# A decoder trunk in one kernel: three layer norms take the form of the last one, with mean and scale left in PSUM

## The chip, the core and the metric

The kernel runs on one core of a Trainium2 chip, as one program in one launch. The core has a matrix engine (PE in the profile, with its weight loads as PEld), VectorE (DVE), ScalarE (ACT), GpSimd (POOL) and a queue for DMAs on SyncE (SP). The metric is the time of one execution on the device in microseconds, and the median over several runs is compared.

## The reference, cut to what matters

Two token groups (256 prompt tokens, and 8 sequences with one token each) go through the same two layers; the kernel keeps all 264 tokens side by side. Each layer has a feed-forward half-step, a mixer and another feed-forward half-step, each followed by a layer norm over 1024 features:

```python
def layer_norm(x, g, b):
    mu = jnp.mean(xf, axis=-1, keepdims=True)
    var = jnp.mean(jnp.square(xf - mu), axis=-1, keepdims=True)
    return ((xf - mu) * lax.rsqrt(var + LN_EPS) * g + b)
...
x = layer_norm(DN_ALPHA * x + 0.5 * swiglu(x, wg1, wu1, wd1), g[0], b[0])
x = layer_norm(DN_ALPHA * x + Mixer(x), g[1], b[1])
x = layer_norm(DN_ALPHA * x + 0.5 * swiglu(x, wg2, wu2, wd2), g[2], b[2])
```

That makes six norms, numbered 0 to 5 here as in the code (`ln`): layer 0 has norms 0, 1 and 2, layer 1 has 3, 4 and 5. The mixer of layer 0 is attention beside an RWKV recurrence, that of layer 1 is a state space (S5) with a gated output projection. Everything is float32.

## The kernel before

Activations lie with features on partitions: 1024 features are 8 blocks (k = 0 to 7) of 128 partitions x 264 tokens. Each float32 product is made of three matmuls on operands that are split into a high and a low part (`block`, lines 297 to 299: high x high, high weight x low activation, low weight x high activation). Weights come from HBM in chunks of up to 8 blocks of 128x128; `Stream.take` loads each ahead and splits it: ScalarE makes the high part (`wh`, line 199), VectorE the low part (`wl`, line 200). So both engines have one large instruction for each chunk all through the kernel, 317 chunks in all. The split chunks lie in 4 buffers, and a new split can start only when PE is done with the oldest.

The order of instructions on each engine is set when the kernel is built: a planner goes through the program with costs of its own, gives instructions that come earlier in the program precedence when several are ready, and writes one fixed order for each engine. On the chip each engine then works through its order and waits wherever an operand isn't there yet. The same source lines therefore can stand in another order at another norm.

How a norm is made. While the projection before it runs, `put_r` (called once for each of the 8 output blocks m) adds the residual to the projection (line 348), takes off a first estimate of the mean, and sums the blocks and their squares in `acc` and `sq`. At the last block four matmuls with a matrix of 1/1024 leave in two PSUM tiles what is still missing of the mean (`dl`) and the mean square (`var`), spread over all partitions (lines 372 and 373). For norms 0, 1, 2 and 4 `put_r` also writes `rh` and `rl`, the two parts of g * r, with r not yet normalised.

Then `stats` makes of these the two factors of the norm. ScalarE squares `dl` (line 394), VectorE takes the square off `var` into the SBUF tile `rstd` (line 396), ScalarE takes the root (line 397) and copies -`dl` into the SBUF tile `nmu` (line 399), VectorE takes the reciprocal in place (line 401). The blocks are centered by `center` (line 437), r + `nmu`: block 0 on VectorE, blocks 1, 2-3, 4-5 and 6-7 on GpSimd in four instructions. Both operands lie in SBUF. Later `unit` (line 448) multiplies a block by `rstd` on VectorE, `norm_block` (line 441) has ScalarE apply g and b, and `split_block` splits the result into `xh` (ScalarE, line 453) and `xl` (VectorE, line 454) for the matmuls.

What hides a norm. `ffn` starts its first three pairs of column blocks (six PSUM banks, `raw`) on `rh` and `rl`, which needs nothing of the norm but r; the factors are put in afterwards on the six finished banks by `fix` (lines 469, 471 and 472: a copy of two columns, `nmu` times one of them plus the bank, and the product with `rstd`). While PE is at these 144 matmuls, the other engines normalise and split the 8 blocks. The fourth pair (`pg`, `pu`) needs `xh` and `xl`, and its bank is that of the first `raw` tile, which line 471 has to have read.

The last norm (5) has nothing to hide behind and goes through `finish`: `dl` and `var` stay in PSUM; ScalarE copies the mean to SBUF for GpSimd, which centers blocks 7, 6 and 5 (line 417); VectorE centers blocks 0 and 1 against `dl` (line 421), writes the reciprocal back into `var` (line 422), and centers blocks 2 to 4 as it comes to them (line 426) before the product with `var` (line 427).

Of the kernel before, what the change touches and what calls it, by code (L numbers as in the profile page):

```python
# [9 lines left out]
F32 = mybir.dt.float32  # L10
# [3 lines left out]
AF = mybir.ActivationFunctionType  # L14
ALU = mybir.AluOpType
# [6 lines left out]
NT = NP + NB  # L22
# [198 lines left out]
class Trunk:  # L221
# [164 lines left out]
        with self.tc.issue_after(after.ins):  # L386
            self.nc.scalar.activation(self.eps[:, 2:3], self.eps[:, 0:1], func)

    def stats(self):

        nc = self.nc
        tt = nc.vector.tensor_tensor
        d2 = self.sp.tile([128, NT], F32, tag="fixt", name="d2", bufs=3)
        nc.scalar.activation(d2, self.dl, AF.Square)
        self.rstd = self.xp.tile([128, NT], F32, tag="rstd", name="rstd")
        self.last_v = tt(out=self.rstd, in0=self.var, in1=d2, op=ALU.subtract)
        nc.scalar.activation(self.rstd, self.rstd, AF.Sqrt, bias=self.eps[:, 0:1])
        self.nmu = self.xp.tile([128, NT], F32, tag="mu", name="nmu")
        nc.scalar.activation(self.nmu, self.dl, AF.Copy, scale=-1.0)
        self.center(0, 1, nc.vector)  # L400
        nc.vector.reciprocal(out=self.rstd, in_=self.rstd)
        self.ws.hold = False
        for k0, k1 in ((1, 2), (2, 4), (4, 6), (6, 8)):
            self.center(k0, k1, nc.gpsimd)

    def finish(self, ln, out):

        nc = self.nc
        dve, pool = nc.vector.tensor_tensor, nc.gpsimd.tensor_tensor
        d2 = self.sp.tile([128, NT], F32, tag="fixt", name="d2", bufs=3)  # L410
        mu = self.sp.tile([128, NT], F32, tag="h", name="mu")
        nc.scalar.copy(mu, self.dl)
        nc.scalar.activation(d2, self.dl, AF.Square)
        v = self.sp.tile([128, NT], F32, tag="fixt", name="v", bufs=3)
        r = lambda k: self.r[:, k, :]
        for k in (7, 6, 5):
            pool(out=r(k), in0=r(k), in1=mu, op=ALU.subtract)
        dve(out=v, in0=self.var, in1=d2, op=ALU.subtract)
        nc.scalar.activation(v, v, AF.Sqrt, bias=self.eps[:, 0:1])
        for k in range(2):  # L420
            dve(out=r(k), in0=r(k), in1=self.dl, op=ALU.subtract)
        nc.vector.reciprocal(out=self.var, in_=v)
        self.new_x(split=False)
        for k in range(KD):
            if 2 <= k < 5:
                dve(out=r(k), in0=r(k), in1=self.dl, op=ALU.subtract)
            dve(out=r(k), in0=r(k), in1=self.var, op=ALU.mult)  # L427
            if k in (4, 7):
                nc.vector.tensor_scalar(out=self.xn[:, k, :], in0=r(k), scalar1=self.g(ln, k), scalar2=self.b(ln, k),
                                        op0=ALU.mult, op1=ALU.add)  # L430
            else:
                nc.scalar.activation(self.xn[:, k, :], r(k), AF.Identity, scale=self.g(ln, k), bias=self.b(ln, k))
            nc.sync.dma_start(out=out[:, k, :], in_=self.xn[:, k, :])

    def center(self, k0, k1, e):
# [8 lines left out]

    def unit(self, k):

        t = self.r[:, k, :]
        self.nc.vector.tensor_tensor(out=t, in0=t, in1=self.rstd, op=ALU.mult)
        return t
# [27 lines left out]
    def ffn(self, layer, f, ln_in, ln_out, raw=True):  # L477
        nc = self.nc
        with ExitStack() as ctx:
            first = ln_in is None  # L480
            self.banks(mm="AABBBC", ms="D", aux="D")
            hp = ctx.enter_context(self.tc.tile_pool(name="hp", bufs=1))
            hh = hp.tile([128, KF, NT], F32R, tag="hh", name="hh")
            hl = hp.tile([128, KF, NT], F32R, tag="hl", name="hl")
            raw_in = ln_in is not None
            ps = [self.ps([128, NO if raw_in else NT], f"raw{i}") for i in range(2 * G1)]
            xh, xl = (self.rh, self.rl) if raw_in else (self.xh, self.xl)
            for k in range(KD):
                if not raw_in:
                    self.split_block(k)  # L490
                for m in range(G1):
                    for i, w in enumerate(("_wg", "_wu")):
                        self.block(ps[2 * m + i], (f + w, layer, k, m), xh[:, k, :], xl[:, k, :], k == 0, k == KD - 1)

            def gate(m, pg, pu):
                sg = self.sp.tile([128, NT], F32, tag="sg", name="sg")
                last = nc.scalar.activation(sg, pg, AF.Silu)
                h = self.sp.tile([128, NT], F32, tag="h", name="h")
                nc.vector.scalar_tensor_tensor(out=h, in0=sg, scalar=0.5, in1=pu, op0=ALU.mult, op1=ALU.mult)  # L499
                self.last = [nc.scalar.copy(hh[:, m, :], h), self.last_mm]  # L500
                self.last_v = nc.vector.tensor_tensor(out=hl[:, m, :], in0=h, in1=hh[:, m, :], op=ALU.subtract)
                self.mark = h[:, 0:1]
                return last

            if not raw_in:
                for m in range(G1):
                    gate(m, ps[2 * m], ps[2 * m + 1])
                with self.tc.issue_after(self.last_v.ins):
                    self.split_vec()
            else:  # L510
                self.new_x()
                done = 0
                for m in range(G1):
                    tg, bg = self.fix(ps[2 * m])
                    tu, bu = self.fix(ps[2 * m + 1])
                    sg = self.sp.tile([128, NT], F32, tag="sg", name="sg")
                    nc.scalar.activation(sg, tg, AF.Silu, bias=bg)
                    h = self.sp.tile([128, NT], F32, tag="h", name="h")
                    nc.vector.scalar_tensor_tensor(out=h, in0=tu, scalar=bu, in1=sg, op0=ALU.add, op1=ALU.mult)
                    nc.scalar.activation(hh[:, m, :], h, AF.Copy, scale=0.5)  # L520
                    nc.vector.scalar_tensor_tensor(out=hl[:, m, :], in0=h, scalar=0.5, in1=hh[:, m, :],
                                                   op0=ALU.mult, op1=ALU.subtract)
                    e = (m + 1) * KD // G1
                    for k in range(done, e):
                        self.norm_block(ln_in, k)
                    done = e
            for m in range(G1, KF):
                pg = self.ps([128, NT], "pg")
                pu = self.ps([128, NT], "pu")
                for ps, w in ((pg, "_wg"), (pu, "_wu")):  # L530
                    for k in range(KD):
                        self.block(ps, (f + w, layer, k, m), self.xh[:, k, :], self.xl[:, k, :], k == 0, k == KD - 1)
                last = gate(m, pg, pu)
                if not raw_in or m % 3:
                    self.advance()
            self.table(AF.Sqrt, last)
            self.new_r(ln_out, raw)
            for m in range(KD):
                ps = self.ps([128, NT], "pd")
                for k in range(KF):  # L540
                    self.block(ps, (f + "_wd", layer, k, m), hh[:, k, :], hl[:, k, :], k == 0, k == KF - 1)
                self.last = self.put_r(ln_out, m, ps) + [self.last_mm]
                if first:
                    self.advance()
                self.ws.hold = m == KD - 2
                if first and m == KD - 2:
                    for _ in self.side:
                        pass
            if ln_out < 5:
                self.stats()  # L550
            else:
                self.finish(ln_out, self.a["y"])

# [51 lines left out]
    def _even(self, ctx, ln_in, ln_out):  # L605
        nc, a, cst = self.nc, self.a, self.cst
# [7 lines left out]
        for i in range(2):  # L614
            h, o = slice(64 * i, 64 * i + 64), slice(64 - 64 * i, 128 - 64 * i)
# [103 lines left out]
        for m in range(KD):  # L719
# [2 lines left out]
            for k in range(4 if m < 4 else 0, 8):  # L722
                self.block(ps, ("w_out_even", 0, k, m), self.oh[:, k, :], self.ol[:, k, :], k == 0, k == 7)
            self.put_r(ln_out, m, ps)
        self.stats()

    def other_half(self, bone, sbb, idb, nmb):

# [911 lines left out]
    def odd(self, ln_in, ln_out):  # L1640
        nc, a = self.nc, self.a
# [3 lines left out]
        with ExitStack() as ctx:  # L1645
# [182 lines left out]
            for m in range(KD):  # L1828
# [9 lines left out]
                if m == KD - 1:  # L1838
# [3 lines left out]
                h = self.sp.tile([128, NT], F32, tag="h", name="mix")  # L1842
                nc.vector.tensor_tensor(out=h[:, :NP].rearrange("p (c j) -> p j c", j=4),
                                        in0=t[:, :NP].rearrange("p (j c) -> p j c", j=4),
                                        in1=po[:, :NP].rearrange("p (j c) -> p j c", j=4), op=ALU.mult)
                nc.vector.tensor_tensor(out=h[:, NP:], in0=t[:, NP:], in1=po[:, NP:], op=ALU.mult)
                self.put_r(ln_out, m, h)
            self.stats()


def trunk(tc, a, order):
# [117 lines left out]
```

## Time and profile before

| | |
|---|---|
| median of 3 runs | 1165.57 us (1163.96 to 1165.69) |
| the profiled execution | 1169.36 us, its span 1167.6 us |
| PE | 1103.8 us busy, 95% of the span |
| VectorE | 871.7 us, 75% |
| ScalarE | 593.0 us, 51% |
| GpSimd | 166.8 us, 14% |

The profile is of one execution. [...] Norm 0 stands at 218 us in the trace, norm 1 at 458, norm 2 at 656, norm 3 at 851, norm 4 at 963 and norm 5 at 1156.

### The profile page before, as it was taken

The page shows a single profiled execution, that of the slowest core. Times are in us where ns is not written, and L with a number is a line of the kernel's source. Part 1 is how long each engine was busy: PE and PEld are TensorE (multiplying, and loading weights), DVE is VectorE, ACT ScalarE, POOL GpSimd, SP SyncE. Part 2 cuts the span into 40 slices and gives each one's busy share as a digit, 9 for nine tenths or more (in the row PEclk, how much of TensorE's full clock was granted, in tenths as well). Part 3 has the DMA queues.
Part 4 walks back from the last instruction along what each step waited for, and adds up shares of the span by engine and source line. Part 5 has one row for each costly group of instructions (what it writes and reads, how often), then busy time and mean ns, then how long its engine had stood idle before and what let it go on. Part 6 is the DMA issues. An engine that isn't in the chain of part 4 may idle for free. (4 is left out here: it accounts for less than half of the span.)

```text
span 1167.6 us, 25704 instructions
## 1 busy us (share of the span) xinstructions
PE 1103.8 (95%) x10391; PEld 1053.5 (90%) x10391; DVE 871.7 (75%) x1726; ACT 593.0 (51%) x1043; POOL 166.8 (14%) x284
## 2 busy tenths in 40 slices
PE   7999999998899989999999999999959999999996
PEld 7999999987787669999999999999948899999995
DVE  4899855879877759888876798675579689555564
ACT  4544554686345435743554654454463366444442
POOL 0000000354445322011200112000020002000000
PEclk9999999999999999999999999999979999999998
DMA  7755656634455424566865567555474353765551
GB/s 255 224 167 159 211 177 219 196 112 123 156 152 170 138 75 147 160 222 216 291 212 181 163 205 219 202 185 176 160 229 129 95 188 123 210 185 184 183 172 49
DMA packets 66119, 204.91 MB, mean 176 GB/s; under 512 B 13464, under 2 KB 16616, under 8 KB 65744
## 3 DMA queue, kind: packets, MB, share of 16 engines
q1 hardware_dynamic: 56400, 174.09, 46.9%
q0 software_dynamic: 6560, 23.27, 6.1%
q10 hardware_dynamic: 3040, 5.92, 1.6%
q8 instruction: 81, 1.33, 0.5%
q14 instruction: 38, 0.31, 0.1%
HBM read 192.22 MB, written 10.86 MB: 174 GB/s over the span
## 5 line engine op out<-in xcount | busy, mean ns | idle before, releaser
L200 DVE TENSOR_TENSOR wl<-raw,wh 128x1024 fp32r<-128x1024 f32 (+2 forms) x317 | 388.2, 1226 | 184.6 <-ACT wh L199 181.7
L199 ACT CAST wh<-raw 128x1024 fp32r<-128x1024 f32 (+2 forms) x317 | 329.8, 1041 | 320.8 <-issue 100.5
L297 PE MATMUL pd<-hh,wh 128*128 128x264 f32 x704 | 200.8, 285 | 0.0
L299 PE MATMUL pd<-hh,wl 128*128 128x264 f32 x704 | 200.7, 285 | 0.0
L298 PE MATMUL pd<-hl,wh 128*128 128x264 f32 x704 | 199.1, 283 | 0.0
L297 PE MATMUL pg<-xh,wh 128*128 128x264 f32 x648 | 184.6, 285 | 5.9 <-DVE fixc L469 4.0
L299 PE MATMUL pg<-xh,wl 128*128 128x264 f32 x648 | 184.2, 284 | 1.3 <-DVE wl L200 1.3
L298 PE MATMUL pg<-xl,wh 128*128 128x264 f32 x648 | 183.8, 284 | 0.0
L299 PE MATMUL pu<-xh,wl 128*128 128x264 f32 x608 | 172.9, 284 | 2.6 <-DVE wl L200 2.6
L297 PE MATMUL pu<-xh,wh 128*128 128x264 f32 x608 | 172.9, 284 | 0.0
L298 PE MATMUL pu<-xl,wh 128*128 128x264 f32 x608 | 172.6, 284 | 0.0
L297 PEld LDWEIGHTS pd<-hh,wh 128*128 128x128 f32 x704 | 132.4, 188 | 0.6
L299 PEld LDWEIGHTS pd<-hh,wl 128*128 128x128 f32 x704 | 132.6, 188 | 0.2
L298 PEld LDWEIGHTS pd<-hl,wh 128*128 128x128 f32 x704 | 132.4, 188 | 0.0
L297 PEld LDWEIGHTS pg<-xh,wh 128*128 128x128 f32 x648 | 122.4, 189 | 6.8 <-ACT xh L453 4.4
L299 PEld LDWEIGHTS pg<-xh,wl 128*128 128x128 f32 x648 | 121.9, 188 | 2.1 <-DVE wl L200 1.9
L298 PEld LDWEIGHTS pg<-xl,wh 128*128 128x128 f32 x648 | 122.4, 189 | 0.0
L299 PEld LDWEIGHTS pu<-xh,wl 128*128 128x128 f32 x608 | 114.3, 188 | 3.5 <-DVE wl L200 3.5
L298 PEld LDWEIGHTS pu<-xl,wh 128*128 128x128 f32 x608 | 115.0, 189 | 0.0
L297 PEld LDWEIGHTS pu<-xh,wh 128*128 128x128 f32 x608 | 114.9, 189 | 0.0
L500 ACT CAST hh<-h 128x264 fp32r<-128x264 f32 x79 | 32.2, 409 | 57.0 <-DVE h L499 57.0
L297 PE MATMUL raw<-rh,wh 128*128 128x266 f32 x192 | 55.9, 291 | 0.1
(548 smaller groups left out, 2159.7 us busy)
## 6 DMA issues: line engine op xcount, KB each, us to landing
raw<-in_w SPq DMA_DIRECT2D x308, 512.0 KB, 3.7
raw<-in_w SPq DMA_DIRECT2D x7, 384.0 KB, 4.7
gxd<-gc SPq DMA_DIRECT2D x8, 256.0 KB, 2.8
qb<-qd POOLq DMA_DIRECT2D x8, 256.0 KB
FT<-wd POOLq DMA_DIRECT2D x8, 256.0 KB
bF<-in_bF POOLq DMA_DIRECT2D x8, 256.0 KB
rot<-rotd ACTq DMA_DIRECT2D x5, 384.0 KB, 3.4
rotd<-T POOLq DMA_DIRECT2D x2, 768.0 KB
```

Source lines behind the costliest of these rows:

```text
L199: nc.scalar.copy(wh[:, :w], raw[:, :w])
L200: nc.vector.tensor_tensor(out=wl[:, :w], in0=raw[:, :w], in1=wh[:, :w], op=ALU.subtract)
L297: mm(ps, lhsT=wh, rhs=xh, start=start, stop=False)
L298: mm(ps, lhsT=wh, rhs=xl, start=False, stop=False)
L299: self.last_mm = mm(ps, lhsT=wl, rhs=xh, start=False, stop=stop)
L500: self.last = [nc.scalar.copy(hh[:, m, :], h), self.last_mm]
```

## The change

`stats` gets an argument `quick`. It is true for norms 1, 2 and 4, whose calls pass it; norms 0 and 3 keep the old form. The first part of `finish` becomes a function of its own, `quick_stats`, which both `finish` and the three norms call. In it ScalarE writes -`dl` into `nmu` ahead of the square (in `finish` this replaces the copy `mu`, so that GpSimd adds where it subtracted); GpSimd centers blocks 7, 6 and 5 in three instructions, VectorE blocks 0 and 1 against `dl` in PSUM, and the reciprocal is written into `var` in PSUM, which becomes `rstd` for `fix` too. The centering of blocks 2 to 4 stands in `quick_unit`, directly ahead of each one's product with `var`.

```diff
@@ -386,8 +386,12 @@
         with self.tc.issue_after(after.ins):
             self.nc.scalar.activation(self.eps[:, 2:3], self.eps[:, 0:1], func)
 
-    def stats(self):
-
+    def stats(self, quick=False):
+
+        self.quick = quick
+        if quick:
+            self.quick_stats()
+            return
         nc = self.nc
         tt = nc.vector.tensor_tensor
         d2 = self.sp.tile([128, NT], F32, tag="fixt", name="d2", bufs=3)
@@ -403,33 +407,45 @@
         for k0, k1 in ((1, 2), (2, 4), (4, 6), (6, 8)):
             self.center(k0, k1, nc.gpsimd)
 
-    def finish(self, ln, out):
+    def quick_stats(self):
 
         nc = self.nc
         dve, pool = nc.vector.tensor_tensor, nc.gpsimd.tensor_tensor
         d2 = self.sp.tile([128, NT], F32, tag="fixt", name="d2", bufs=3)
-        mu = self.sp.tile([128, NT], F32, tag="h", name="mu")
-        nc.scalar.copy(mu, self.dl)
+        self.nmu = self.xp.tile([128, NT], F32, tag="mu", name="nmu")
+        nc.scalar.activation(self.nmu, self.dl, AF.Copy, scale=-1.0)
         nc.scalar.activation(d2, self.dl, AF.Square)
         v = self.sp.tile([128, NT], F32, tag="fixt", name="v", bufs=3)
         r = lambda k: self.r[:, k, :]
         for k in (7, 6, 5):
-            pool(out=r(k), in0=r(k), in1=mu, op=ALU.subtract)
+            pool(out=r(k), in0=r(k), in1=self.nmu, op=ALU.add)
         dve(out=v, in0=self.var, in1=d2, op=ALU.subtract)
         nc.scalar.activation(v, v, AF.Sqrt, bias=self.eps[:, 0:1])
         for k in range(2):
             dve(out=r(k), in0=r(k), in1=self.dl, op=ALU.subtract)
-        nc.vector.reciprocal(out=self.var, in_=v)
+        self.last_v = nc.vector.reciprocal(out=self.var, in_=v)
+        self.rstd = self.var
+        self.ws.hold = False
+
+    def quick_unit(self, k):
+        r, dve = self.r[:, k, :], self.nc.vector.tensor_tensor
+        if 2 <= k < 5:
+            dve(out=r, in0=r, in1=self.dl, op=ALU.subtract)
+        dve(out=r, in0=r, in1=self.var, op=ALU.mult)
+        return r
+
+    def finish(self, ln, out):
+
+        nc = self.nc
+        self.quick_stats()
         self.new_x(split=False)
         for k in range(KD):
-            if 2 <= k < 5:
-                dve(out=r(k), in0=r(k), in1=self.dl, op=ALU.subtract)
-            dve(out=r(k), in0=r(k), in1=self.var, op=ALU.mult)
+            r = self.quick_unit(k)
             if k in (4, 7):
-                nc.vector.tensor_scalar(out=self.xn[:, k, :], in0=r(k), scalar1=self.g(ln, k), scalar2=self.b(ln, k),
+                nc.vector.tensor_scalar(out=self.xn[:, k, :], in0=r, scalar1=self.g(ln, k), scalar2=self.b(ln, k),
                                         op0=ALU.mult, op1=ALU.add)
             else:
-                nc.scalar.activation(self.xn[:, k, :], r(k), AF.Identity, scale=self.g(ln, k), bias=self.b(ln, k))
+                nc.scalar.activation(self.xn[:, k, :], r, AF.Identity, scale=self.g(ln, k), bias=self.b(ln, k))
             nc.sync.dma_start(out=out[:, k, :], in_=self.xn[:, k, :])
 
     def center(self, k0, k1, e):
@@ -444,6 +460,8 @@
 
     def unit(self, k):
 
+        if self.quick:
+            return self.quick_unit(k)
         t = self.r[:, k, :]
         self.nc.vector.tensor_tensor(out=t, in0=t, in1=self.rstd, op=ALU.mult)
         return t
@@ -547,7 +565,7 @@
                     for _ in self.side:
                         pass
             if ln_out < 5:
-                self.stats()
+                self.stats(ln_out == 2)
             else:
                 self.finish(ln_out, self.a["y"])
 
@@ -722,7 +740,7 @@
             for k in range(4 if m < 4 else 0, 8):
                 self.block(ps, ("w_out_even", 0, k, m), self.oh[:, k, :], self.ol[:, k, :], k == 0, k == 7)
             self.put_r(ln_out, m, ps)
-        self.stats()
+        self.stats(True)
 
     def other_half(self, bone, sbb, idb, nmb):
 
@@ -1845,7 +1863,7 @@
                                         in1=po[:, :NP].rearrange("p (j c) -> p j c", j=4), op=ALU.mult)
                 nc.vector.tensor_tensor(out=h[:, NP:], in0=t[:, NP:], in1=po[:, NP:], op=ALU.mult)
                 self.put_r(ln_out, m, h)
-            self.stats()
+            self.stats(True)
 
 
 def trunk(tc, a, order):
```

## Rows read from the trace of the kernel before

**Rows 1.** The page, busy time, share of the span and instructions, PE.

```profile
PE 1103.8 (95%) x10391; PEld 1053.5 (90%) x10391; DVE 871.7 (75%) x1726; ACT 593.0 (51%) x1043; POOL 166.8 (14%) x284
```

**Rows 2.** All waits of PE: for what, us in total, times, longest.

```profile
PE pg L297 <- DVE fixc L469: 4.0, 2, 2.2
...
PE pg L297 <- DVE fixt L471: 0.5, 1, 0.5
```

**Rows 3.** Two stretches: length, busy us and instructions by engine, PEclk, DMA share, GB/s.

```profile
473.00:485.00 12.00, 9.78 (x68) 9.60 (x67) 10.44 (x29) 7.82 (x15) 0.33 (x2) 0.86 0.29 87
976.50:988.00 11.50, 9.70 (x80) 9.52 (x79) 10.53 (x29) 8.88 (x16) 0.00 (x0) 1.00 0.30 94
```

**Rows 4.** PE in order of time after norm 1: start, us, line, operation [idle before].

```profile
473.28 0.28 PE L299 MATMUL raw<-rh,wl 128*128 128x266 f32 x1
475.77 0.36 PE L297 MATMUL pg<-xh,wh 128*128 128x264 f32 x1 [2.22 <-DVE fixc L469]
...
477.46 0.42 PE L297 MATMUL pg<-xh,wh 128*128 128x264 f32 x1
477.68 0.42 PE L298 MATMUL pg<-xl,wh 128*128 128x264 f32 x1
```

**Rows 5.** PE in order of time after norm 2.

```profile
673.35 0.36 PE L297 MATMUL pg<-xh,wh 128*128 128x264 f32 x1 [0.53 <-DVE fixt L471]
```

**Rows 6.** PE in order of time after norm 4.

```profile
979.24 0.36 PE L297 MATMUL pg<-xh,wh 128*128 128x264 f32 x1 [1.80 <-DVE fixc L469]
```

**Rows 7.** VectorE in order of time at norm 1.

```profile
458.11 0.43 DVE L437 TENSOR_TENSOR r<-r,nmu 128x264 f32<-128x264 f32 x1
...
461.88 4.19 DVE L200 TENSOR_TENSOR wl<-raw,wh 128x1024 fp32r<-128x1024 f32 x2
466.00 2.14 DVE L448 TENSOR_TENSOR r<-r,rstd 128x264 f32<-128x264 f32 x6
468.06 1.21 DVE L200 TENSOR_TENSOR wl<-raw,wh 128x1024 fp32r<-128x1024 f32 x1
...
474.00 1.23 DVE L200 TENSOR_TENSOR wl<-raw,wh 128x1024 fp32r<-128x1024 f32 x1 [0.92 <-ACT wh L199]
475.14 0.48 DVE L471 SCALAR_TENSOR_TENSOR fixt<-nmu,fixc,raw 128x264 f32<-128x264 f32 x1
```

**Rows 8.** ScalarE in order of time at norm 1.

```profile
466.46 0.61 ACT L441 ACTIVATE xn<-r,vec 128x264 f32<-128x264 f32 x1 [3.80 <-DVE r L448]
...
472.94 1.03 ACT L199 CAST wh<-raw 128x1024 fp32r<-128x1024 f32 x1
```

**Rows 9.** GpSimd in order of time at norms 1, 2 and 4.

```profile
458.16 6.83 POOL L437 TENSOR_TENSOR r<-r,nmu 128x264 f32<-128x264 f32 x4 [26.75 <-ACT nmu L399]
...
655.40 5.14 POOL L437 TENSOR_TENSOR r<-r,nmu 128x264 f32<-128x264 f32 x4 [65.88 <-ACT nmu L399]
...
962.81 6.79 POOL L437 TENSOR_TENSOR r<-r,nmu 128x264 f32<-128x264 f32 x4 [49.53 <-ACT nmu L399]
```

**Rows 10.** VectorE in order of time at norm 4.

```profile
966.61 1.81 DVE L200 TENSOR_TENSOR wl<-raw,wh 128x1024 fp32r<-128x1024 f32 x1
968.35 3.26 DVE L448 TENSOR_TENSOR r<-r,rstd 128x264 f32<-128x264 f32 x6
...
977.47 1.23 DVE L200 TENSOR_TENSOR wl<-raw,wh 128x1024 fp32r<-128x1024 f32 x1 [0.91 <-ACT wh L199]
```

**Rows 11.** VectorE in order of time at norm 2.

```profile
658.49 2.34 DVE L448 TENSOR_TENSOR r<-r,rstd 128x264 f32<-128x264 f32 x2
...
672.71 0.89 DVE L471 SCALAR_TENSOR_TENSOR fixt<-nmu,fixc,raw 128x264 f32<-128x264 f32 x2
```

**Rows 12.** Durations of single lines: count, ns min/median/max, first and last start, forms.

```profile
L448 DVE TENSOR_TENSOR r<-r,rstd x40: 420/422/1555, 221.4 to 974.0; 128x264 f32<-128x264 f32 x40
...
L427 DVE TENSOR_TENSOR r<-r,var x8: 414/420/421, 1159.5 to 1162.8; 128x264 f32<-128x264 f32 x8
...
L417 POOL TENSOR_TENSOR r<-r,mu x3: 742/743/748, 1156.2 to 1157.6; 128x264 f32<-128x264 f32 x3
```

## The prediction

> **What bounds the kernel now.** The page first: PE is busy 95% of the span [rows 1], so the other engines count only where PE stops for them. Then the waits of PE: among them are three at the fourth pair of column blocks (`pg`) of a feed-forward half-step, put down to the `fix` lines 469 and 471 [rows 2], together 4.5 us. Third, PE in order of time behind the three norms that change: it stands for 2.22 us after norm 1, 0.53 after norm 2 and 1.80 after norm 4 [rows 4 to 6]. Behind the first stop comes a second price: the matmuls then start 0.22 us apart and take 0.42 us [rows 4], and the granted clock is 0.86 over those 12 us, while after norm 4, with the shorter stop, it is 1.00 [rows 3]. [...] So the most that a faster norm can give back here is 2.22 + 1.7 + 0.53 + 1.80 = 6.2 us, 0.5% of the time.
>
> Why PE stands there is read from VectorE, followed back from line 471, whose end lets PE go on. After norm 1 it starts at 475.14, behind a `wl` at 474.00 that VectorE had waited 0.92 us for, because ScalarE began its `wh` only at 472.94 [rows 7, 8]. ScalarE was late because it had stood 3.80 us for the first normalised block, until 466.46 [rows 8]. That block was late because VectorE spent 4.19 us on two `wl` ahead of it, where one alone takes 1.21 [rows 7], in a stretch in which GpSimd centered, from 458.16 on for 6.83 us [rows 9]. So the chain is: GpSimd's centering beside VectorE's instructions with two SBUF operands, a late first block, ScalarE behind, `wl` behind, line 471 behind, PE. Norm 4 shows the same: six products of line 448 take 3.26 us there and 2.14 at norm 1, after GpSimd had ended [rows 7, 9, 10].
>
> **The change part by part.** All of it beside PE's `raw` matmuls; on the path to the end lies only what moves line 471.
>
> *GpSimd centers three blocks, not seven.* Alone a block takes it 0.742 us [rows 12], so three take about 2.2 us in place of 6.83, 5.14 and 6.79 [rows 9]. In those first 2.2 us VectorE's planned work is mostly the variance, two centerings from PSUM and the reciprocal. What VectorE gets back is what its instructions lost: at norm 1, 4.19 - 2 x 1.21 = 1.8 us on two `wl`; at norm 4, 3.26 - 2.14 = 1.1 on six products and 1.81 - 1.21 = 0.6 on a `wl`, together 1.7; at norm 2, two products took 2.34 instead of 2 x 2.14 / 6 = 0.71, so 1.6 [rows 7, 10, 11]. Bounds: all of this, or nothing, if a `wl` comes to stand beside each of the three instructions that stay. I take all of it, because the stretched rows stand after the third GpSimd block would have ended.
>
> *VectorE centers five blocks, not one.* Four more instructions. With `dl` and `var` in PSUM the nearest rows are line 427 of the last norm: 414 to 421 ns, and line 448 with both operands in SBUF has 420 to 422 at the least and the middle [rows 12]; back to back, six take 2.14 us, 0.357 each [rows 7]. So 4 x 0.357 = 1.4 us are added to each norm, 0.36 of it (block 1) ahead of the first product. The products with `var` in PSUM and line 472 in `fix` I cost at nothing more by the same rows. They also can't be held by GpSimd, as far as the last norm shows: its three GpSimd instructions stayed within 742 to 748 ns.
>
> [...]
>
> *Order of `nmu` and the square.* The two ScalarE copies change places, so the variance can start when both are done, which is when VectorE's first centering started before (458.11, [rows 7]). GpSimd starts one copy earlier. I cost it at nothing; the bounds are one short instruction either way, 0.4 us, hidden as far as ScalarE and VectorE are behind by a `wl` anyway.
>
> *PSUM held longer.* `dl` and `var` keep their two banks until line 472 has run for the sixth `raw` bank. The next user of those banks is the mean estimate of the following down projection, some hundred matmuls later. No cost; and the last norm, which runs the same instructions as before, doesn't change.
>
> *The sum.* Norm 1: VectorE gets 1.8 back and pays 1.4, so it is 0.4 us ahead when the `raw` banks come; it stood ready 0.92 us before the `wl` of 474.00, at 473.08, so now at 472.7. The first block reaches ScalarE 1.8 - 0.36 = 1.4 us earlier, and ScalarE was behind from there on, so its `wh` ends at 474.0 - 1.4 = 472.6. The `wl` starts at the later of the two, 472.7, and line 471 and PE come 1.3 us earlier. The stop shrinks from 2.22 to 0.9 us, less than the 1.80 that left the clock at 1.00 after norm 4: so 1.7 us of lower clock go too. Norm 4: VectorE 1.7 - 1.4 = 0.3 ahead, ready at 977.47 - 0.91 - 0.3 = 976.3; `wh` 1.7 - 0.36 = 1.3 earlier, 976.2; gain 1.2 us. Norm 2: VectorE 1.6 - 1.4 = 0.2 ahead at line 471 (672.71, [rows 11]), of a stop of 0.53; I take 0.3, since ScalarE's earlier start helps some. Together 1.3 + 1.7 + 1.2 + 0.3 = 4.5 us. What is late next is the same line 471, by 0.9 us after norm 1 and 0.6 after norm 4; then the low parts `xl` of the last blocks, which follow it in VectorE's order and move with it. Behind the stops PE works without a pause, so what is won there stays won.
>
> The profiled execution took 1169.36 us (span 1167.6 and 1.8 around it), 0.3% more than the median of the runs, 1165.57. The sum is taken off both: 1164.9 for a profiled execution, 1161.1 for the median.
>
> **The rivals.**
>
> *Only part of it* (0.2). The planner gives the instructions another order, in which the eight products and three centerings stand together ahead of the `wl`, or `wl` stands beside GpSimd's three blocks. Speaks for it: the order differs between norms 1 and 2 for the same lines (six products in a row, two in a row; [rows 7, 11]). Against it: at both norms 1 and 4 a reserve of 0.9 us lies in VectorE's wait for `wh`. Price: half of the three stops' 2.8 us, with the clock kept (1.7) or not: 1162.5 to 1164.2.
>
> *Nothing to see* (0.15). The wait is really for the `raw` banks and the order at line 471, and a `wl` stands ahead of it whatever comes earlier. For it: PE's stop is put down to lines of `fix`, not to `xh` [rows 2]. Against it: that `wl` itself waited [rows 7, 10]. Time: 1164.5 to 1166.5.
>
> *VectorE becomes the bound of the norm, slower* (0.13). Nothing comes back, because GpSimd's three blocks now meet `wl`, and the 1.4 us of added centerings all stand ahead of line 471. It decides where what VectorE gets back is under 1.4 - 0.9 = 0.5 us. Then line 471 comes 0.5 us later after norms 1 and 4, and up to 1.4 after norm 2; the stop after norm 4 grows to 2.3 us, over the 2.22 behind which the clock fell, which costs another 1.7: 1165.57 + 0.5 + 0.5 + 1.4 + 1.7 = 1169.7 at the worst, 1168 with half of norm 2. For it: VectorE is dense from the variance to the `raw` banks. Against it: the last norm's rows [rows 12].
>
> *PSUM operands are dear* (0.02). Some 18 instructions a norm (8 products, 4 centerings more, 6 in `fix`), each longer by the difference between line 471, which reads a bank, and line 427: 0.48 - 0.42 = 0.06 us; about 12 of them stand ahead of the first line 471, 0.7 us. Then VectorE is 0.3 behind instead of 0.4 ahead at norm 1, still inside its 0.92: gains 0.6, 0.5, 0 and the clock's 1.7, so 1162.8. [...]
>
> **How the numbers follow.** The forecast (gain over 3.2 us) has 0.5, with its own range from 1159.4 (all 6.2 us) to 1162.4. "Faster" by over 0.2%, 2.3 us, about the least that a measurement of this kernel tells from no change (its three runs spread over 1.7 us), takes 0.5, half of the second case and most of the last: 0.61. "Slower" is the fourth case, 0.13. The rest is within: 0.26. The range goes from 1159 to 1167, which leaves out the worst of the slower case and little below.
>
> **What would show it.** Line 437 gone at norms 1, 2 and 4; GpSimd at work about 2.2 us in each; no `wl` of the norm over 1.5 us and no product over 0.5; the first `xn` of norm 1 about 1.4 us earlier after the sums are done; PE's stop after norm 1 under 1 us and the granted clock 1.00 there. It is wrong if a `wl` stretches beside GpSimd as before, if VectorE no longer waits for `wh` yet line 471 comes no earlier, or if the stops go and PE loses as much at another place.

## The result: 1181.8 us, 1.2% slower

The changed kernel takes 1181.79 us (median of 5 runs, 1179.92 to 1183.06), the kernel before 1165.69 beside it: ratio 1.0118, with a 95% interval of 1.0099 to 1.0138. Forecast were 1161.1 us, in a range from 1159 to 1167. The profiled execution took 1181.79 us with a span of 1180.0, against 1169.36 and 1167.6.

### The profile page after: what moved, and what is told of

It is laid out like the page before. It is cut to its first block, busy times and chain, and to the rows that moved or that the text cites. A ratio compares the mean times of both kernels' runs of the same rounds, so it can differ in the third digit from the quotient of the medians.

```text
span 1180.0 us, 25711 instructions
## 1 busy us (share of the span) xinstructions
PE 1108.8 (94%) x10391; PEld 1058.0 (90%) x10391; DVE 869.6 (74%) x1738; ACT 594.6 (50%) x1043; POOL 162.6 (14%) x281
## 5 line engine op out<-in xcount | busy, mean ns | idle before, releaser
L200 DVE TENSOR_TENSOR wl<-raw,wh 128x1024 fp32r<-128x1024 f32 (+2 forms) x317 | 385.7, 1218 | 199.2 <-ACT wh L199 195.4
L299 PE MATMUL pd<-hh,wl 128*128 128x264 f32 x704 | 200.7, 285 | 0.0
L421 POOL TENSOR_TENSOR r<-r,nmu 128x264 f32<-128x264 f32 x12 | 10.9, 937 | 338.0 <-ACT nmu L416 338.0
```

Of the source, the lines that this page charges most:

```text
L200: nc.vector.tensor_tensor(out=wl[:, :w], in0=raw[:, :w], in1=wh[:, :w], op=ALU.subtract)
L299: self.last_mm = mm(ps, lhsT=wl, rhs=xh, start=False, stop=stop)
L421: pool(out=r(k), in0=r(k), in1=self.nmu, op=ALU.add)
```

## The profile after

The busy line of the page, which answers to [rows 1]: PE is busy 5 us longer with the same 10391 matmuls, yet its share of the longer span is smaller; VectorE and GpSimd are busy for less time than before.

```profile
PE 1108.8 (94%) x10391; PEld 1058.0 (90%) x10391; DVE 869.6 (74%) x1738; ACT 594.6 (50%) x1043; POOL 162.6 (14%) x281
```

All waits of PE, the lines that answer to [rows 2]. The three stops of 4.5 us together are now three of 4.46 each, and they are no longer put down to `fix` on VectorE but to the high parts of the normalised blocks on ScalarE (lines moved by 18: `xh` was 453).

```profile
PE pg L297 <- ACT xh L471: 13.4, 3, 4.5
```

PE in order of time at the end of the 144 `raw` matmuls and behind them (start in us from the start of the span, us, operation, and in brackets the idle time before it with what ended it), for [rows 4], and three windows with PEclk, the clock granted to PE as a share of its full speed, in the third column from the end, for [rows 3]. The reader is to see a stop of 4.46 us, matmuls 0.22 us apart in place of 0.12 for 4.7 us behind it (from 477.4 to 482.1, with a granted clock of 0.50), and the same at norms 2 and 4, where the clock had been 1.00 before (672 to 684 us for norm 2, [rows 3] for norm 4): it now stands at 0.72 over the 12 us of all three.

```profile
472.63 0.28 PE L299 MATMUL raw<-rh,wl 128*128 128x266 f32 x1
477.37 0.59 PE L297 MATMUL pg<-xh,wh 128*128 128x264 f32 x1 [4.46 <-ACT xh L471]
...
477.97 0.42 PE L297 MATMUL pg<-xh,wh 128*128 128x264 f32 x1
478.19 0.42 PE L298 MATMUL pg<-xl,wh 128*128 128x264 f32 x1
...
482.14 0.28 PE L298 MATMUL pu<-xl,wh 128*128 128x264 f32 x1
482.26 0.29 PE L299 MATMUL pu<-xh,wl 128*128 128x264 f32 x1
```

```profile
472.90:485.00 12.10, 7.64 (x46) 7.63 (x46) 11.94 (x34) 9.30 (x20) 0.33 (x2) 0.72 0.26 85
674.70:687.00 12.30, 7.84 (x49) 7.76 (x49) 12.10 (x35) 9.49 (x20) 0.34 (x2) 0.72 0.30 84
984.70:997.00 12.30, 7.84 (x47) 7.72 (x46) 12.10 (x35) 9.46 (x20) 0.00 (x0) 0.72 0.27 82
```

VectorE in order of time at norm 1, for [rows 7]. Two things stand side by side in it. The two `wl` behind the reciprocal take 2.33 us where they took 4.19, as forecast. And the eight products (line 434) don't follow: the three centerings of line 433 do, then VectorE stands idle 1.74 and 1.78 us, waiting for `wh` of the next chunks, and only behind the two `fix` of the first round (lines 487, 489, 490) come two products, at 473.81. Before, the first six were at work at 466.00.

```profile
457.41 0.43 DVE L425 TENSOR_TENSOR r<-r,dl 128x264 f32<-128x264 f32 x1
...
461.50 2.33 DVE L200 TENSOR_TENSOR wl<-raw,wh 128x1024 fp32r<-128x1024 f32 x2
463.75 1.10 DVE L433 TENSOR_TENSOR r<-r,dl 128x264 f32<-128x264 f32 x3
465.03 1.23 DVE L200 TENSOR_TENSOR wl<-raw,wh 128x1024 fp32r<-128x1024 f32 x1 [0.17 <-ACT wh L199]
467.99 1.22 DVE L200 TENSOR_TENSOR wl<-raw,wh 128x1024 fp32r<-128x1024 f32 x1 [1.74 <-ACT wh L199]
470.99 1.22 DVE L200 TENSOR_TENSOR wl<-raw,wh 128x1024 fp32r<-128x1024 f32 x1 [1.78 <-ACT wh L199]
...
472.32 0.89 DVE L489 SCALAR_TENSOR_TENSOR fixt<-nmu,fixc,raw 128x264 f32<-128x264 f32 x2
473.13 0.76 DVE L490 TENSOR_TENSOR fixt<-fixt,var 128x264 f32<-128x264 f32 x2
473.81 0.76 DVE L434 TENSOR_TENSOR r<-r,var 128x264 f32<-128x264 f32 x2
```

ScalarE in order of time for [rows 8]: its first normalised block starts at 475.61, 9 us later than at 466.46, and its `xh`, which PE waits for, at 476.92. Its order changed with VectorE's. The first product is done at 474.2 (473.81 and 0.42 us for one), but the load of a function table (1.28 us) and the `sg` of the first `fix` now stand ahead of the block; before, the load came behind all eight blocks, at 476.88. So about 1.4 us of the stop are ScalarE's.

```profile
473.89 1.28 ACT L535 ACT_TABLE_LOAD   x1
475.19 0.51 ACT L535 ACTIVATE sg<-fixt,fixc 128x264 f32<-128x264 f32 x1
475.61 1.09 ACT L457 ACTIVATE xn<-r,vec 128x264 f32<-128x264 f32 x2
476.61 0.41 ACT L538 ACTIVATE hh<-h 128x264 fp32r<-128x264 f32 x1
476.92 0.71 ACT L471 CAST xh<-xn 128x264 fp32r<-128x264 f32 x2
```

The load in the kernel before:

```profile
476.88 1.28 ACT L517 ACT_TABLE_LOAD   x1
```

GpSimd at norm 1, for [rows 9], and the products' durations in the whole program, for [rows 12]:

```profile
457.17 3.19 POOL L421 TENSOR_TENSOR r<-r,nmu 128x264 f32<-128x264 f32 x3 [26.45 <-ACT nmu L416]
```

```profile
L434 DVE TENSOR_TENSOR r<-r,var x32: 417/423/428, 473.8 to 1175.3; 128x264 f32<-128x264 f32 x32
```

GpSimd is done after 3.2 us in place of 6.8, where 2.2 were forecast, and a product with its scale in PSUM takes 423 ns, as forecast. The prices of VectorE's instructions hold; the order of its queue is what changed.

## How the runs are compared

Ahead of norm 1 the kernels don't differ in their source (but for experiment 7, which changes norm 0), yet the profiled executions reach it between 451 and 463 us, with a granted clock from 0.89 to 1.00 between 340 and 400 us. From there on they repeat closely. So beside each median the table gives, from one profile, the time from the start of the matmuls that close `var` at norm 1 (line 373, the first of two) to the same point at norm 2, from norm 2 to 3, 3 to 4, and from norm 4 to the end of the span. A kernel that was profiled twice agrees within 0.1 us in the sum.

| kernel | median us | ratio to before (95%) | 1 to 2 | 2 to 3 | 3 to 4 | 4 to end | sum |
|---|---|---|---|---|---|---|---|
| before | 1165.69 | 1 | 197.3 | 194.9 | 112.4 | 205.5 | 710.1 |
| changed | 1181.79 | 1.0118 (1.0099 to 1.0138) | 199.9 | 201.0 | 111.7 | 210.5 | 723.1 |
| 1, scale in SBUF | 1159.74 | 0.9934 (0.9913 to 0.9955) | 194.0 | 194.5 | 112.0 | 203.8 | 704.3 |
| the same again | 1157.22 | 0.9953 (0.9925 to 0.9982) | 194.1 | 194.5 | 111.8 | 203.8 | 704.2 |
| 2, `fix` reads a copy | 1161.24 | 0.9954 (0.9937 to 0.9971) | 195.0 | 194.6 | 111.6 | 204.6 | 705.8 |
| 3, before + scale in PSUM | 1180.57 | 1.0098 (1.0066 to 1.0130) | 200.0 | 200.7 | 111.7 | 210.4 | 722.8 |
| 4, products written first | 1165.43 | 0.9971 (0.9948 to 0.9993) | 194.8 | 194.5 | 111.7 | 204.4 | 705.4 |
| 5, order forced, SBUF | 1179.01 | 1.0092 (1.0062 to 1.0123) | 200.2 | 201.2 | 111.7 | 210.6 | 723.7 |
| 6, centering from SBUF | 1166.47 | 0.9985 (0.9963 to 1.0007) | 197.8 | 195.3 | 111.9 | 204.9 | 709.9 |
| the same again | 1161.59 | 0.9979 (0.9964 to 0.9993) | 197.6 | 195.4 | 111.9 | 204.9 | 709.8 |
| 7, all norms | 1161.88 | 0.9944 (0.9915 to 0.9973) | 194.0 | 194.5 | 112.9 | 203.7 | 705.1 |
| 8, PSUM at norm 1 only | 1168.22 | 1.0006 (0.9982 to 1.0029) | 199.9 | 194.5 | 111.7 | 203.8 | 709.9 |
| 9, no GpSimd | 1161.42 | 0.9976 (0.9961 to 0.9991) | 195.9 | 194.4 | 111.7 | 205.0 | 707.0 |

The runs came in three groups, the last on another chip, in which the kernel before had medians of 1168.1 (1 to 4), 1167.8 (5 to 8) and 1164.4 us (the two repeats and 9); so ratios and stretches are to be compared, not medians of different groups. Where the intervals of two ratios overlap, as those of 6 and 9 do with that of the repeat of 1, the difference is read from the stretches alone.

## The experiments

The theory that these rows suggest: the planner holds the readers of one PSUM tile in the order of the program. `fix` and the products both read `var`, and in the program the first `fix` stands ahead of the first product. With `rstd` in SBUF the planner had let the products pass. (In this kernel's source the matmuls leave their sums in PSUM and take their operands from SBUF.)

**Experiment 1: scale back in SBUF, all else as changed.**

```diff
-        self.last_v = nc.vector.reciprocal(out=self.var, in_=v)
-        self.rstd = self.var
+        self.rstd = self.var if last else self.xp.tile([128, NT], F32, tag="rstd", name="rstd")
+        self.last_v = nc.vector.reciprocal(out=self.rstd, in_=v)
...
-        dve(out=r, in0=r, in1=self.var, op=ALU.mult)
+        dve(out=r, in0=r, in1=self.rstd, op=ALU.mult)
```

> Theory: the loss is the order of the products on VectorE. With the scale in PSUM, `fix` and the products read one PSUM tile, and the planner keeps the readers of a PSUM tile in the order of the program, where `fix` (which needs finished `raw` banks) stands first. With the reciprocal in SBUF again and all else as changed, the products stand ahead of `fix`, and the gain that was forecast appears: 1160 to 1164 us, PE's three stops under 1 us each. Rival A (five centerings and eight products are too much for VectorE, so they slip): the work is the same, so the stops stay near 4.5 us and the time near 1181. Rival B (an instruction with a PSUM operand is dear or waits): the products get better but the centerings against dl stay, so in between, about 1172.

Measured: 1159.74 us, a little under the range that was expected, ratio 0.9934. VectorE in order of time at norm 1, and the one wait of PE for `xh` that is left (line numbers as in the changed kernel):

```profile
456.98 2.29 DVE L200 TENSOR_TENSOR wl<-raw,wh 128x1024 fp32r<-128x1024 f32 x2
459.19 0.77 DVE L434 TENSOR_TENSOR r<-r,rstd 128x264 f32<-128x264 f32 x2
...
467.66 0.22 DVE L487 COPY fixc<-raw 128x2 f32<-128x2 f32 x2
...
468.65 0.77 DVE L490 TENSOR_TENSOR fixt<-fixt,rstd 128x264 f32<-128x264 f32 x2
```

```profile
PE pg L297 <- ACT xh L471: 0.6, 1, 0.6
```

The first products start at 459.19, right behind the two `wl`, 6.8 us after the sums of norm 1; in the changed kernel it was 16.9. As the theory has it; rival A and rival B fall. The wait of 0.6 us is not at the start of the fourth pair: it comes 9 us later, at the eighth block, whose product stands behind all `fix` in this kernel too. The repeat was expected at 1158 to 1163 us and at 704 to 706 from norm 1 on; it took 1157.22, just under, and 704.2.

**Experiment 2: the products read PSUM, `fix` a copy.**

```diff
             self.quick_stats()
+            self.rstd = self.xp.tile([128, NT], F32, tag="rstd", name="rstd")
+            self.nc.scalar.copy(self.rstd, self.var)
```

> Scale in PSUM for the products as changed; `fix` reads a copy of it in SBUF that ScalarE makes (one instruction more for each norm). Theory: the tie between `fix` and the products is gone, so 1160 to 1165 us, though every product still reads PSUM. Rival A: 1181. Rival B: the products still read PSUM, so near 1181 too.

Measured: 1161.24 us, ratio 0.9954, 705.8 us from norm 1 on. All products still read PSUM, and the loss is gone: the first products start 6.9 us after the sums (457.1), and PE's waits for `xh` come to 1.0 us.

```profile
463.98 0.76 DVE L436 TENSOR_TENSOR r<-r,var 128x264 f32<-128x264 f32 x2
```

```profile
PE pg L297 <- ACT xh L473: 1.0, 2, 0.6
```

The 1.5 us over experiment 1 lie at norms 1 and 4 (195.0 and 204.6). ScalarE has the copy to make there, but at norm 2 as well; that the copy is the cause isn't shown.

**Experiment 3: the kernel before with nothing but the scale in PSUM.**

```diff
-        nc.vector.reciprocal(out=self.rstd, in_=self.rstd)
+        if quick:
+            nc.vector.reciprocal(out=self.var, in_=self.rstd)
+            self.rstd = self.var
+        else:
+            nc.vector.reciprocal(out=self.rstd, in_=self.rstd)
```

> The kernel before with one edit: at norms 1, 2 and 4 the reciprocal is written into the PSUM tile, which products and `fix` read. GpSimd centers seven blocks, VectorE one, as before. Theory: nearly the whole loss, 1178 to 1183 us, with products behind `fix` and PE stopped for over 4 us at each of the three. Rival A: VectorE has no more to do than before, so 1166. Rival B: 1170 to 1181.

Measured: 1180.57 us, ratio 1.0098, 722.8 us from norm 1 on: the whole loss from one operand's place. PE's wait, and VectorE in order of time (line 476 is `fix`, 452 the products):

```profile
PE pg L297 <- ACT xh L457: 13.4, 3, 4.5
```

```profile
473.58 0.76 DVE L476 TENSOR_TENSOR fixt<-fixt,var 128x264 f32<-128x264 f32 x2
474.26 0.76 DVE L452 TENSOR_TENSOR r<-r,var 128x264 f32<-128x264 f32 x2
```

**Experiment 4: the changed kernel with the products written ahead of `fix`.**

```diff
                 self.new_x()
                 done = 0
+                if self.quick:
+                    for k in range(KD):
+                        self.unit(k)
                 for m in range(G1):
```

(and `norm_block` then takes the finished block.)

> The changed kernel with one edit: the eight products (with the centerings of blocks 2 to 4) are written ahead of the first `fix` in the program; the scale stays in PSUM for both. Theory: the readers keep the order of the program, and it is now the wanted one, so 1160 to 1167 us. Rival A and rival B: 1181, since amount and kind of the work are unchanged.

Measured: 1165.43 us, ratio 0.9971, 705.4 us from norm 1 on. VectorE at norm 1: all eight products (line 435) now stand ahead of the first `fix` (492), with the scale in PSUM for both.

```profile
466.93 2.34 DVE L200 TENSOR_TENSOR wl<-raw,wh 128x1024 fp32r<-128x1024 f32 x2
469.18 0.77 DVE L435 TENSOR_TENSOR r<-r,var 128x264 f32<-128x264 f32 x2
...
472.62 1.10 DVE L435 TENSOR_TENSOR r<-r,var 128x264 f32<-128x264 f32 x3
...
474.79 0.76 DVE L435 TENSOR_TENSOR r<-r,var 128x264 f32<-128x264 f32 x2
...
478.68 0.76 DVE L492 TENSOR_TENSOR fixt<-fixt,var 128x264 f32<-128x264 f32 x2
```

The same instructions on the same operands, in another order of the program, and 17.7 us less from norm 1 on. That the planner takes the order from the program is thereby shown, and not only that PSUM has to do with it.

**Experiment 5: that order with the scale in SBUF.** An order edge puts each product of experiment 1 behind the `fix` before it; no product and no `fix` reads `var`.

```diff
-        dve(out=r, in0=r, in1=self.rstd, op=ALU.mult)
+        with ExitStack() as c:
+            if self.fixed is not None:
+                c.enter_context(self.tc.issue_after(self.fixed.ins))
+            dve(out=r, in0=r, in1=self.rstd, op=ALU.mult)
```

> The first experiment's kernel (scale in SBUF) with an order edge: each product must stand behind the `fix` instructions that precede it in the program. No product reads PSUM. Theory (the order is the loss, not where the operand lies): all of the loss again, 1178 to 1183 us, PE stopped for about 4.5 us at each of norms 1, 2 and 4. Rival (a PSUM operand costs by itself): 1160 to 1170.

Measured: 1179.01 us, ratio 1.0092, and the stretches of the changed kernel within 0.3 us. PE's wait, and VectorE's order (495 is `fix`, 438 the products):

```profile
PE pg L297 <- ACT xh L476: 13.4, 3, 4.5
```

```profile
457.96 2.29 DVE L200 TENSOR_TENSOR wl<-raw,wh 128x1024 fp32r<-128x1024 f32 x2
460.17 1.10 DVE L434 TENSOR_TENSOR r<-r,dl 128x264 f32<-128x264 f32 x3
...
469.59 0.77 DVE L495 TENSOR_TENSOR fixt<-fixt,rstd 128x264 f32<-128x264 f32 x2
470.28 0.77 DVE L438 TENSOR_TENSOR r<-r,rstd 128x264 f32<-128x264 f32 x2
```

So the order alone costs all of it, 723.7 us from norm 1 on with the scale in SBUF against 723.1 with it in PSUM; where the operand lies costs nothing beside that.

**Experiment 8: scale in PSUM at norm 1 only.** Experiment 1 with `quick_stats` told to write `var` at that one norm.

> The first experiment's kernel with the scale in PSUM at norm 1 only. Theory: each norm pays for itself, about a third of what lies between the changed kernel and the first experiment (about 20 us), so 6 to 7 us over the first experiment, near 1166, with one stop of 4.5 us after norm 1 and none after norms 2 and 4. Rival (the loss comes once, from the order of the whole program): near 1160 or near 1180.

Measured: 1168.22 us; the stretch from norm 1 to 2 takes 199.9 us as in the changed kernel, the others are those of experiment 1. One stop:

```profile
PE pg L297 <- ACT xh L471: 4.5, 1, 4.5
```

Each norm pays for itself: 5.9 us at norm 1, and from the table 6.5 at norm 2 and 6.7 at norm 4. Of the 5.9, PE's waits for `xh` grew by 4.5 - 0.6 = 3.9; the matmuls behind the stop, for 4.7 us 0.22 us apart in place of 0.12 in the changed kernel, lost about 4.7 x (0.22 - 0.12) / 0.22 = 2.1 there (an estimate from those rows), so the two cover it.

**Experiment 6, run twice: centering from SBUF.** This asks where the gain comes from that experiment 1 has over the kernel before. VectorE's five centerings use `nmu` in place of `dl`.

```diff
-            dve(out=r(k), in0=r(k), in1=self.dl, op=ALU.subtract)
+            dve(out=r(k), in0=r(k), in1=self.dl if last else self.nmu, op=ALU.subtract if last else ALU.add)
...
-            dve(out=r, in0=r, in1=self.dl, op=ALU.subtract)
+            dve(out=r, in0=r, in1=self.nmu, op=ALU.add)
```

> The first experiment's kernel, VectorE's five centerings taken from `nmu` in SBUF in place of dl in PSUM. Theory (an instruction with two SBUF operands is held up beside GpSimd): the first two centerings meet GpSimd's three, some stretch to over 0.6 us, the norm starts 0.3 to 1 us later, hidden or nearly: 1159 to 1163. Rival (what the changed form gains comes only from GpSimd having three blocks, and from no operand's place): the same time as the first experiment and no centering over 0.5 us. Second rival (PSUM operands carry most of the gain): 1165 or more.

> The sixth experiment's kernel (VectorE's centerings from SBUF) once more. Its first profile had a weight transfer that came late at norm 1. Theory now (PSUM operands carry most of the gain, since the centerings and the `wl` beside GpSimd stretch): 4 to 7 us over the kernel above, stretched centerings at all three norms, and the stop after norm 1 again over 1 us. Rival (that late transfer was chance and made most of the difference): 1 to 3 us over it.

Measured: 1166.47 and 1161.59 us, ratios 0.9985 and 0.9979; beside experiment 1 on the same chip 4.4 us more, and 5.6 us more from norm 1 on (709.8 to 704.2), which leaves 0.3 us of the gain over before. My first number (1159 to 1163) missed; that a centering stretches was right, and so was the second rival. VectorE at norm 1 in the two repeats, first with `nmu` in SBUF, then with `dl` in PSUM:

```profile
453.81 0.98 DVE L425 TENSOR_TENSOR r<-r,nmu 128x264 f32<-128x264 f32 x1
454.71 0.42 DVE L422 TENSOR_TENSOR v<-var,d 128x264 f32<-128x264 f32 x1
455.05 0.65 DVE L425 TENSOR_TENSOR r<-r,nmu 128x264 f32<-128x264 f32 x1
455.62 1.77 DVE L200 TENSOR_TENSOR wl<-raw,wh 128x1024 fp32r<-128x1024 f32 x1
```

```profile
451.57 0.43 DVE L425 TENSOR_TENSOR r<-r,dl 128x264 f32<-128x264 f32 x1
451.92 0.43 DVE L422 TENSOR_TENSOR v<-var,d 128x264 f32<-128x264 f32 x1
452.26 0.42 DVE L425 TENSOR_TENSOR r<-r,dl 128x264 f32<-128x264 f32 x1
452.60 1.31 DVE L200 TENSOR_TENSOR wl<-raw,wh 128x1024 fp32r<-128x1024 f32 x1
```

0.98 and 0.65 us against 0.43 and 0.42, and the `wl` behind takes 1.77 against 1.31: about 1.2 us at once. PE's stops at the fourth pair are back, with 1.5, 1.0 and 1.4 us at norms 1, 2 and 4 in the repeat. So in these runs GpSimd's shorter share alone brings next to nothing (0.3 us from norm 1 on), and VectorE's centerings with an operand from PSUM keep 0.42 to 0.43 us while GpSimd is at work (in the repeat of experiment 1 from 451.34 on for 3.18 us). How much of the 5.6 us is this stretching stays open: in both profiles with `nmu` ScalarE also waited for a weight transfer at norm 1, 2.52 and 2.61 us, and the planner gave this kernel another order (its eighth product stands ahead of `fix`, that of experiment 1 behind).

**Experiment 9: no GpSimd at the three norms.** VectorE centers all eight blocks against `dl`.

> The first experiment's kernel without GpSimd at norms 1, 2 and 4: VectorE centers all eight blocks from PSUM. VectorE gets three instructions more for each norm (1.1 us) and nothing is held up any more (about 0.2 us back on a `wl`). Theory (the gain came from GpSimd's being away while VectorE splits, and VectorE still has some reserve): within 2 us of the first experiment, 1160 to 1163. Rival (GpSimd's three blocks are still needed): the stops come back, 1164 to 1167.

Measured: 1161.42 us, 4.2 more than experiment 1 beside it, 2.8 more from norm 1 on, with two stops where experiment 1 has one of 0.6:

```profile
PE pg L297 <- ACT xh L471: 2.4, 2, 1.3
```

The time lies in the range that the theory named, but beside its neighbour it is the rival's stops that show, if not its time: one after norm 1 (1.3 us) and one after norm 4 (1.1), where VectorE has three instructions more, 1.1 us a norm. At norm 2, with the same three, nothing is lost. GpSimd's three blocks are still worth 2.8 us.

**Experiment 7: the form of experiment 1 at norms 0 and 3 too.** `stats(ln_out == 2)` becomes `stats(True)`.

> The first experiment's kernel with the new form at norms 0 and 3 as well. Theory: norm 0 has no stop of PE behind it, so nothing comes of it; at norm 3 PE waits 8.7 us for a transfer that begins with the normalised blocks, and VectorE's two centerings more ahead of the first product cost what GpSimd's shorter work gives back: within 1.5 us of the first experiment. Rival: norm 3 lies open, and its products come up to 1.5 us earlier, so 1 to 3 us faster.

Measured: 1161.88 us, ratio 0.9944; 705.1 us from norm 1 on. Norm 3 to 4 takes 112.9 in place of 111.8 to 112.0: nothing is won there. Norm 0 lies ahead of the stretches that repeat, so these runs show nothing of it.

Experiment 1 beats both kernels, by 0.66% and in the repeat 0.47% under the kernel before.

## Why the prediction was wrong, point by point

*What bounds the kernel* was right, and so was the chain behind the three stops. From norm 1 on, experiment 1 has the forecast's terms nearly one by one: 3.2 to 3.3 us at norm 1 (forecast 1.3 of stop and 1.7 of clock), 0.4 at norm 2 (0.3), 1.7 at norm 4 (1.2), with 0.4 to 0.6 elsewhere: 5.8 to 5.9 against 4.5. The 1.7 us of clock, in this sum as in the bound of 6.2 and in the rivals' prices, is a term that no run shows. In its place the kernel before shows a granted clock of 0.50 from 477.1 to 480.4 us, with matmuls 0.22 us apart in place of 0.12, so 3.3 x (0.22 - 0.12) / 0.22 = 1.5 us (an estimate from those rows), and experiment 1 a clock of 1.00 from 470 to 500. The stop after norm 1, said to shrink to 0.9 us, is gone from the start of the fourth pair, and 0.6 us of waiting came at another place, the eighth block.

*VectorE centers five* holds in durations, *GpSimd centers three blocks* nearly: it was at work for 3.2 us at norms 1 and 4 and 2.4 at norm 2, not 2.2. I put the gain down to GpSimd's shorter share and the PSUM operands as a side note ("can't be held by GpSimd, as far as the last norm shows"); experiment 6 turns that round: without the PSUM operands nearly nothing is left of the gain (0.3 of 5.9 us).

*The step that failed* is the sentence "The products with `var` in PSUM and line 472 in `fix` I cost at nothing more by the same rows", with "No cost" for holding `var` until line 472. The rows it rests on [rows 12] give an instruction's duration, and that was right (423 ns). What they can't give is the order: at the last norm no `fix` reads `var`, so nothing there stands ahead of the products. At norms 1, 2 and 4 `var` has a second group of readers, `fix`, which needs the finished `raw` banks, comes first in the program, and so held all eight products until the 144 matmuls that were to hide them were over (the last starts at 472.63, the first product at 473.81). The stops, said to shrink under the 1.80 us that had left the clock at 1.00, grew to 4.46, and with each the clock stood at 0.72 over 12 us. Price: 18.8 us from norm 1 on (723.1 - 704.3), where I had written nothing; 704.3 is what the rest of the change gives.

*The rivals.* "VectorE becomes the bound, slower" named the right sign with the wrong cause: VectorE stands idle over 1.7 us twice in the stretch in which it was to be too full. (By its own terms it comes to 1169.0 with half of norm 2, not 1168.) "Only part of it" spoke of another order by the planner, but of one drawn from free choice, priced at 1.4 to 3.1 us; that an edit could tie two groups of instructions was in none of them. *PSUM operands are dear* is refuted by experiment 2, where two products from PSUM take 0.76 us against 0.77 for two from SBUF in experiment 1; its price was no PSUM price either, since lines 471 and 427, whose difference it took, both read PSUM. *Nothing to see* falls with experiment 1, in which earlier products brought most of the stops' time back.

What experiments 1 to 4 show of this kernel's planner is that it holds two groups of readers of a PSUM tile on one engine, reads against reads (first product 16.9 us after the sums with the scale in PSUM, 6.8 with it in SBUF).

## What to carry to other kernels

Before a value moves to PSUM, list who else reads it and where each reader stands in the program: under a planner that keeps such readers in order, an early reader with a late operand holds back all that come after it. A row from another place in the kernel gives the duration of an instruction, not the place it will get in its queue; for that, ask what the planner will hold it behind. And give each group of readers its own tile (SBUF for the products, or a copy), which here turned a loss of 1.2% into a gain of 0.5 to 0.7%.

## What the runs showed of the hardware that was not expected

In the rows that follow, GpSimd and VectorE hold each other up, and the one that starts second takes longer. In experiment 1 GpSimd's three centerings at norm 1 took 771, 781 and 1752 ns (least, middle and most in the row below); alone one takes 742 [rows 12]. The long one, the last, started at 454.11, 0.19 us behind a `wl` at 453.92 that itself took only 1.32 us instead of 1.22. The `wl` ended at 455.24, and the centering at 455.86, 0.62 us later. In the repeat of experiment 6 GpSimd started first, at 453.73, and VectorE's centering at 453.81 took 0.98 us. VectorE's own instructions with an operand in PSUM kept their 0.42 to 0.43 us beside GpSimd in the rows of experiment 6.

```profile
L421 POOL TENSOR_TENSOR r<-r,nmu x3: 771/781/1752, 452.7 to 454.1; 128x264 f32<-128x264 f32 x3
```

The granted clock went with the length of a stop in most rows: 1.80 us left it at 1.00 [rows 3], 2.22 us came with 0.86 over 12 us, and 4.46 us came with 0.72 over 12 us at all three norms of the changed kernel. Length alone doesn't settle it: in experiment 3 the stops after norms 1, 2 and 4 are of 4.5 us each, and the clock over 30 us was 0.89 (470 to 500), 0.94 (670 to 700) and 0.89 (970 to 1000).
